# Moving the turned h and the list of further blocks in a mixture-of-experts loop

## The chip, the cores and the metric

The kernel runs on one core of a Trainium2 chip. The metric is the device time of one execution in microseconds (us). Before the change it is 3120.03 us, the median of three runs (3110.61, 3120.03 and 3121.97).

The engines have these names in the profile: PE is TensorE (matmuls; PEld its weight loads; PEq its sequencer, which takes instructions and branches), DVE is VectorE, ACT is ScalarE, POOL is GpSimd and SP is SyncE, which issues most DMAs here.

## The reference, cut to what matters

One block of a hybrid network over 2048 tokens of 1024 channels: a modulated norm, four token mixers side by side, their gated sum, and then a mixture of experts. Only the last part is touched by the change:

```
def hier_moe(h, rg_w, rg_b, re_w, re_b, w1, w3, w2):
    g_logits = hf @ rg_w + rg_b                     # 4 groups
    p_group = the softmax of the best group
    e_logits = (hf @ re_w + re_b) of that group     # 8 experts each
    top_v, top_i = lax.top_k(e_in, 2)
    w = p_group * softmax(top_v)
    return grouped_experts(h, expert ids, w, w1, w3, w2)

def expert_block(xb, e):                            # in blocks of rows of one expert
    return (silu(xb @ w1[e]) * (xb @ w3[e])) @ w2[e]   # 1024 -> 512 -> 1024

y[token] = the weighted sum over the token's two experts
out = rms_norm(x + gate * y)
```

There are 32 experts, and 2 x 2048 assignments of tokens to them, 128 for each on average. How many rows an expert gets is known only when the kernel runs.

## The kernel before, in words

The function `ffn` routes the tokens, makes for each expert the list of its rows (`idx`, `sct`) and their count (`cnt`), and then runs over the experts. The loop (L1053) is written out: 32 experts and one more pass that ends the last one. Matmuls that must be exact to fp32 are done in three passes: each operand is split into a high and a low part (`mhi` by ScalarE at L1294, `mlo` by VectorE at L1295), and `mm3` (L1434) issues low x high, high x low and high x high (L1438 to L1440).

The rows of an expert are worked in three sizes:

- The first 128 rows, always: gathered from `FR` (L869), turned by transposes (`parts`, L883), then `up` (48 matmuls into `ps_mm`), `silu`, `gate` (L928), turned again, and `down` (24 matmuls into `ps_sc`), whose result is multiplied at L949 and added to the output by an indirect DMA (L931).
- The next 64 rows, the *small block*, in two halves of 32, each behind a guard (`tc.If(count > 128 + 32 j)`): `up_rest` is its first product and `down_rest` its second (both `quarters`, matmuls at L958 into `ps_hf`, guard at L956); `placed_rest` multiplies (L987) and scatters behind the guard at L991. The guards are taken by TensorE and GpSimd (`ENGINES`). The count comes into their registers by `values_load` (L1038), two experts ahead.
- Rows beyond 192 of an expert go to a loop behind all experts (L1114), one block of 128 rows each. `beyond` (L1004 to L1032) makes the list of these blocks with VectorE alone.

The order in which the work of one pass of the loop is written, for expert e: [turned h of expert e-1: four transposes (L880), the copy of the high part by ScalarE (L891), the low part by VectorE (L892); split of w2 of expert e-1]; the load of the count of e+2; `up_rest`(e); `up`(e); silu; gate of the small block (L978) and its turning; turned rows of e+1; gate; gathers for e+2; `down`(e-1); `down_rest`(e); `placed_rest`(e). The helper `in_order` (L821) chains all instructions of TensorE, ScalarE and VectorE within the loop in that written order; so a step that is written earlier stands earlier on each of the three engines. DMAs, GpSimd's and SyncE's instructions are placed by the compiler's scheduler, and so is what stands ahead of the loop.

Weights stream in as panels of 128x1024 (`mraw`, 16 buffers; `mhi` and `mlo`, 12 each).

Of the kernel before, what the change touches and what calls it, by code (L numbers as in the profile page):

```python
# [4 lines left out]
F32 = mybir.dt.float32  # L5
F32R = mybir.dt.float32r
BF = mybir.dt.bfloat16
I32 = mybir.dt.int32
AF = mybir.ActivationFunctionType
OP = mybir.AluOpType  # L10
AX = mybir.AxisListType
# [550 lines left out]
NE, FF = 32, 512  # L562
CAP = 2048
NSLOT = 2
FIT = 192
# [5 lines left out]
def ffn(tc, G, A, out, bcast, rsqrt, split, mm3, MT, MR, X1, FR, mid):  # L571
    nc = tc.nc
# [4 lines left out]
    i32_ = rp.tile([128, 32], F32, name="i32_")  # L577
# [5 lines left out]
    cnt = rp.tile([128, 32], F32, name="cnt")  # L583
# [21 lines left out]
    with tc.tile_pool(reuse_waits="tile", name="wo", bufs=1, side="right") as wop, \  # L605
# [59 lines left out]
        def turned(i, x1, f, ss_, lg):  # L665
            fT = fTs[order.index(i) % 3].rearrange("p (k t) -> p k t", t=128)
            for c, o in enumerate(H):
                nc.vector.scalar_tensor_tensor(f[:, o], x1[:, o], ss_[:, 3:4], a4[:, o], op0=OP.mult, op1=OP.mult)
                nc.vector.tensor_add(f[:, o], f[:, o], m3[:, o])
                pt = psum("tr")  # L670
                for k in range(4):
                    nc.tensor.transpose(pt[:, k * 128:(k + 1) * 128], f[:, (4 * c + k) * 128:(4 * c + k + 1) * 128], G.ident)
                nc.scalar.copy(fT[:, 4 * c:4 * c + 4].rearrange("p k t -> p (k t)"), pt)
            for k in range(2):
                nc.sync.dma_start(FR[k * T + i * 128:k * T + (i + 1) * 128, 0:D], f)
            return fT, lg
# [119 lines left out]
        listed = assign(idx, sct, tab.rearrange("p s e -> p (s e)"), at, own)  # L796
# [16 lines left out]
    def parted(raw, eng=nc.vector):  # L813

        hi, lo = (wr.tile([128, 1024], F32R, name=n, bufs=PARTS) for n in ("mhi", "mlo"))
        split(raw, hi, lo, eng)
        return hi, lo, raw
# [3 lines left out]
    def in_order():  # L821

        traced = nc.cur_bb.bb.instructions
        if queues.get("block") is not traced:
            queues.clear()
            queues.update(block=traced, at=len(traced))
        for i in traced[queues["at"]:]:
            if i.engine in (mybir.EngineType.PE, mybir.EngineType.Activation, mybir.EngineType.DVE):
                if i.engine in queues:
                    tc.add_manual_dep(i, queues[i.engine].name, mybir.DependencyInfo(  # L830
                        mybir.DependencyClass.NoSync, mybir.DependencyReason.DATA), reason="in order")
                queues[i.engine] = i
        queues["at"] = len(traced)
# [13 lines left out]

    G.banks(mm=2, tr=2, sc=2, hf0=1, hf1=1)
    hu, hd = (psum(f"hf{i}") for i in range(2))
    for p in (hu, hd):  # L850
        nc.vector.memset(p, 0.0)

    xgs = [wr.tile([128, D + 1], F32, name=f"xg{r}") for r in (128, 64)]
    for i, x in enumerate(xgs):
# [28 lines left out]
    def parts(src, n, name):  # L883

        hi, lo = (wp.tile([128, n, 128], F32R, name=name + c) for c in "hl")
        out = []
        turned_into(lambda *a: out.append(a), src, 128, n)

        def taken():
            for c, v in out:  # L890
                nc.scalar.copy(hi[:, c], v)  # L891
                nc.vector.tensor_sub(lo[:, c], v, hi[:, c].bitcast(F32))  # L892
        return taken, (hi, lo)
# [8 lines left out]
    def weights(xg):  # L902
        w = wp.tile([128, 1], F32, name="w0", bufs=2)
        nc.scalar.copy(w, xg[:, D:D + 1])  # L904
        return w

    def weights_rest(xg):

        w = wp.tile([64, 2], F32, name="w1", bufs=2)
        for j, h in product(range(2), range(2)):  # L910
            nc.scalar.copy(w[h * 32:h * 32 + 32, j:j + 1], xg[j * 32:j * 32 + 32, D:D + 1])
        return w
# [67 lines left out]
    def down_rest(h, w2, guard):  # L980
        quarters(hd, 4, guard, lambda k, j: h[:, j * 2 + k % 2, (k // 2) * 32:(k // 2) * 32 + 32],
                 lambda k, g: w2[k][:, g * 256:g * 256 + 256])
# [19 lines left out]
    ovp = mo.enter_context(tc.tile_pool(reuse_waits="tile", name="ov", bufs=1))  # L1002

    def beyond():  # L1004

        J = -(-(CAP - FIT) // 128)
        ov = ovp.tile([128, 32], F32, name="ov")
        thr = ovp.tile([128, J], F32, name="thr")
        nc.vector.tensor_scalar(thr, i32_[:, :J], 128.0, float(FIT), op0=OP.mult, op1=OP.add)
        le = wp.tile([128, OVB, 32], BF, name="le", tag="mh1")  # L1010
        gt = le[:, :, :J]
        nc.vector.tensor_tensor(gt, cnt.unsqueeze(2).to_broadcast([128, 32, J]), thr.unsqueeze(1).to_broadcast([128, 32, J]),
                                op=OP.is_gt)
        nc.vector.tensor_reduce(ov, gt, axis=AX.X, op=OP.add)
        inc = ov
        for k in range(5):
            nxt = ovp.tile([128, 32], F32, name=f"inc{k}")
            nc.vector.tensor_copy(nxt[:, :1 << k], inc[:, :1 << k])
            nc.vector.tensor_add(nxt[:, 1 << k:], inc[:, 1 << k:], inc[:, :32 - (1 << k)])
            inc = nxt  # L1020
        nc.vector.tensor_tensor(le, inc.unsqueeze(1).to_broadcast([128, OVB, 32]),
                                i32_.unsqueeze(2).to_broadcast([128, OVB, 32]), op=OP.is_le)
        ej = ovp.tile([128, OVB], F32, name="ej")
        nc.vector.tensor_reduce(ej, le, axis=AX.X, op=OP.add)
        nc.vector.tensor_tensor(le, le, ov.unsqueeze(1).to_broadcast([128, OVB, 32]), op=OP.mult)
        bj = ovp.tile([128, OVB], F32, name="bj")
        nc.vector.tensor_reduce(bj, le, axis=AX.X, op=OP.add)
        nc.vector.tensor_sub(bj, i32_, bj)
        nc.vector.tensor_copy(ovt[:, 0:OVB], ej)
        nc.vector.tensor_copy(ovt[:, 2 * OVB:], inc[:, 31:32])  # L1030
        nc.vector.tensor_scalar(ej, ej, float(CAP), float(FIT), op0=OP.mult, op1=OP.add)
        nc.vector.scalar_tensor_tensor(ovf, bj, 128.0, ej, op0=OP.mult, op1=OP.add)  # L1032

    def fetch(e_, guard):
        return gather(idx[:, e_:e_ + 1], 0, nullcontext), gather(idx[0:64, NE + e_:NE + e_ + 1], 1, guard)
# [7 lines left out]
    out1, x1 = plain(rows_[1], 8, "xq", hd)  # L1043
    out0(), out1()
    w, w1 = weights(rows_[0]), weights_rest(rows_[1])
    rows_ = fetch(1, lambda: guards[1](0))
    sct4 = wr.tile([128, NE, 2], I32, name="sct4")
    for g, j in product(range(4), range(2)):
        nc.gpsimd.tensor_scalar(sct4[g * 32:g * 32 + 32, :, j], sct[j * 32:j * 32 + 32, NE:], 4.0, float(g), op0=OP.mult, op1=OP.add)
    with tc.issue_after(listed.ins):  # L1050
        w13 = [parted(t, nc.gpsimd if u < 2 else nc.vector) for u, t in enumerate(in_panels(0))]
    w2n = w2 = None
    for e_ in range(NE + 1):  # L1053
        in_order()
        more = e_ + 1 < NE
        q = nc.sync if e_ else nc.gpsimd
        if e_:

            turned, h = parts(h, 4, "h")
            turned()  # L1060
            in_order()
            w2, w2n = [parted(t) for t in w2n], None
            in_order()
        if e_ < NE:
            guard = guards[e_]
            if e_ + 2 < NE:
                guards.append(over(load(e_ + 2)))

            up_rest(x1, w13[:4], w13[4:], guard)
            pa = up(x, w13[:4], w13[4:])  # L1070
            in_order()
            raw = in_panels(e_ + 1, q) if more else []
            w2n = [loaded(A["e2"][e_][:, u], q) for u in range(4)]
            n13 = [parted(t) for t in raw[:4]]
            hn, h1 = silu(pa), silu_rest()
            in_order()
            gate_rest(h1, w1)
            out1, t1 = plain(h1, 4, "hq", hu)
            n13 += [parted(t) for t in raw[4:7]]
            out1()  # L1080
            if more:
                out0, x = parts(rows_[0], 8, "x")
                out1, x1 = plain(rows_[1], 8, "xq", hd)
                out0()
            in_order()
            gate(pa, hn, w)
            n13 += [parted(t) for t in raw[7:]]
            if more:
                out1()
                w, w1 = weights(rows_[0]), weights_rest(rows_[1])  # L1090
                if e_ + 2 < NE:
                    rows_ = fetch(e_ + 2, lambda: guards[e_ + 2](0))
            in_order()
        if e_:
            placed(down(h, [w2] * 2), sct[:, e_ - 1:e_], rest)
            in_order()
        if e_ < NE:
            down_rest(t1, w2n, guard)
            rest = placed_rest(guard, e_)
            in_order()  # L1100
            h, w13 = hn, n13
            if not more:
                beyond()


    fn, *e = [rp.tile([128, D], F32, name="mraw") for _ in range(RAW)]
# [7 lines left out]
    with tc.For_i(0, nov, 1) as it:  # L1114
# [4 lines left out]
        for k in range(2):  # L1119
            dlt = wp.tile([128, N], F32, name="ovd")  # L1120
            nc.vector.tensor_scalar(dlt, slot[k], sb, None, op0=OP.subtract)
            for i in range(N):
                P = wp.tile([128, 128], BF, name="ovP")
                for c in range(4):
                    nc.vector.tensor_scalar(P[:, c * 32:(c + 1) * 32], i32_, dlt[:, i:i + 1], float(-c * 32),
                                            op0=OP.subtract, op1=OP.is_equal)
# [10 lines left out]
        w2 = [InTurn(lambda u: dy("e2")[:, u], otiles) for _ in range(2)]  # L1137
# [5 lines left out]
        h = silu(pa)  # L1143
# [518 lines left out]
```

## Time and profile before

| | |
|---|---|
| median of three runs | 3120.03 us |
| profiled execution | 3115.34 us |
| its span (first to last instruction) | 3113.5 us |
| mean granted clock of TensorE | 0.958 |
| TensorE busy | 2822.9 us (91%) |
| VectorE busy | 1839.2 us (59%) |
| ScalarE busy | 1154.0 us (37%) |

The shares are means over stages with different limits. The stages from 0 to about 2223 us are the mixers and the router, which the change leaves as they are; from about 2223 to 3062 us run the loop's start, the 32 experts (some 25 us each) and the last `down`; after that the output is read again, normed and written. In a row of the order of time the first number is the start from the span's start, the second the duration, and the bracket at its end tells how long the engine stood before it and what it was waiting for.

### The profile page before, as it was taken

What the parts mean: (1) busy time and instruction counts of PE and PEld (TensorE: products, weight loads), DVE (VectorE), ACT (ScalarE), POOL (GpSimd) and SP (SyncE); (2) the same over time, 40 slices, a digit from 0 to 9 for tenths busy, and PEclk for the clock granted to TensorE, in tenths of its full rate; (3) what the DMA queues carried; (4) which work ended last, traced back from release to release, by engine and by line L of the source; (5) the groups of instructions that cost most, each with busy time, mean ns of one, the idle gap of its engine ahead of it and who ended that gap; (6) DMA issues with size and microseconds to landing.
All of it is one profiled execution on the core that took longest, in us unless ns stands there. A gap on an engine that the chain in (4) does not pass through costs nothing. (4 is left out here: it accounts for less than half of the span.)

```text
span 3113.5 us, 43212 instructions
## 1 busy us (share of the span) xinstructions
PE 2822.9 (91%) x15893; PEld 2229.4 (72%) x15893; DVE 1839.2 (59%) x2870; ACT 1154.0 (37%) x1722; POOL 574.3 (18%) x522
## 2 busy tenths in 40 slices
PE   7999999999967999899999999999688999999992
PEld 3887887787755677777777777887466767776671
DVE  4625125978776478523335333566588777787674
ACT  5411122322336133132222222322366566666552
POOL 3300010000004121013334333100211222111211
PEclk8999999999978899999999999999799999999996
DMA  7736254423118476866335433655698889998786
GB/s 288 252 111 214 80 166 146 155 86 95 68 43 267 130 213 195 268 230 236 122 125 181 160 115 133 195 177 162 198 331 296 287 291 299 307 319 289 251 270 232
DMA packets 245981, 621.46 MB, mean 200 GB/s; under 512 B 31128, under 2 KB 81464, under 8 KB 242008
## 3 DMA queue, kind: packets, MB, share of 16 engines
q1 hardware_dynamic: 211312, 506.17, 46.9%
q0 software_dynamic: 34416, 111.88, 12.8%
q8 instruction: 163, 2.67, 0.3%
q14 instruction: 90, 0.74, 0.1%
HBM read 484.86 MB, written 137.28 MB: 200 GB/s over the span
## 5 line engine op out<-in xcount | busy, mean ns | idle before, releaser
L1295 DVE TENSOR_TENSOR mlo<-mraw,mhi 128x1024 fp32r<-128x1024 f32 x382 | 450.2, 1225 | 58.5 <-ACT mhi L1294 53.0
L1294 ACT CAST mhi<-mraw 128x1024 fp32r<-128x1024 f32 x384 | 383.6, 1047 | 84.3 <-issue 44.7
L1438 PE MATMUL ps_mm<-hb1h,wlo 128*128 128x512 f32 x800 | 320.0, 400 | 3.7 <-DVE wlo L1295 3.7
L1440 PE MATMUL ps_mm<-hb1h,whi 128*128 128x512 f32 x800 | 318.3, 398 | 0.0
L1439 PE MATMUL ps_mm<-hb1l,whi 128*128 128x512 f32 x800 | 318.3, 398 | 0.0
L1589 ACT ACTIVATE ev<-ps_mm 128x512 f32<-128x512 f32 x128 | 76.2, 597 | 618.5 <-PE ps_mm L1440 515.6
L1295 DVE TENSOR_TENSOR wlo<-wraw,whi 128x1024 fp32r<-128x1024 f32 x164 | 217.2, 1333 | 142.6 <-ACT whi L1294 142.4
L1438 PE MATMUL ps_mm<-hb0h,wlo 128*128 128x512 f32 x672 | 269.5, 401 | 16.0 <-DVE wlo L1295 12.5
L1439 PE MATMUL ps_mm<-hb0l,whi 128*128 128x512 f32 x672 | 269.7, 401 | 0.0
L1440 PE MATMUL ps_mm<-hb0h,whi 128*128 128x512 f32 x672 | 267.8, 398 | 0.0
L1294 ACT CAST whi<-wraw 128x1024 fp32r<-128x1024 f32 x176 | 182.2, 1045 | 163.8 <-PE ps_mm L1440 70.0
L1438 PE MATMUL ps_mm<-mhi,xl 128*128 128x512 f32 x512 | 205.7, 402 | 24.5 <-PEq L956 24.2
L1639 POOL TENSOR_TENSOR macc<-macc,ev 128x512 f32<-128x512 f32 x96 | 167.1, 1740 | 307.0 <-DVE ev L1638 304.0
L1638 DVE TENSOR_TENSOR ev<-ev,ps_tr 128x512 f32<-128x512 f32 x96 | 65.8, 687 | 248.7 <-PE ps_tr L1440 243.8
L1439 PE MATMUL ps_mm<-mlo,xh 128*128 128x512 f32 x512 | 202.4, 395 | 3.2 <-ACT mhi L1294 2.4
L1440 PE MATMUL ps_mm<-mhi,xh 128*128 128x512 f32 x512 | 201.8, 394 | 1.4 <-issue 1.4
L1438 PEld LDWEIGHTS ps_mm<-hb1h,wlo 128*128 128x128 f32 x800 | 151.5, 189 | 38.2 <-DVE wlo L1295 4.1
L1440 PEld LDWEIGHTS ps_mm<-hb1h,whi 128*128 128x128 f32 x800 | 151.3, 189 | 33.1 <-issue 2.4
L1439 PEld LDWEIGHTS ps_mm<-hb1l,whi 128*128 128x128 f32 x800 | 151.4, 189 | 32.4 <-issue 1.9
L1438 PEld LDWEIGHTS ps_mm<-hb0h,wlo 128*128 128x128 f32 x672 | 127.7, 190 | 45.7 <-DVE wlo L1295 14.1
L869 POOL DMA_INDIRECT xg<-d_FR,idx x48 | 67.5, 1406 | 459.4 <-ACT w L904 444.1
L1439 PEld LDWEIGHTS ps_mm<-hb0l,whi 128*128 128x128 f32 x672 | 127.9, 190 | 29.5 <-issue 3.4
(592 smaller groups left out, 5861.0 us busy)
## 6 DMA issues: line engine op xcount, KB each, us to landing
mraw<-e SPq DMA_DIRECT2D x372, 512.0 KB
wraw<-wg SPq DMA_DIRECT2D x80, 512.0 KB
wraw<-wt SPq DMA_DIRECT2D x40, 512.0 KB
aw<-adaw SPq DMA_DIRECT2D x64, 256.0 KB
d_GS<-ev SPq DMA_DIRECT2D x64, 256.0 KB
ev<-d_GS POOLq DMA_DIRECT2D x64, 256.0 KB, 4.3
wraw<-wg POOLq DMA_DIRECT2D x24, 512.0 KB, 3.9
d_FR<-hb0h SPq DMA_DIRECT2D x22, 512.0 KB
```

Source lines behind the costliest of these rows:

```text
L869: nc.gpsimd.indirect_dma_start(out=xg, out_offset=None, in_=FR, in_offset=bass.IndirectOffsetOnAxis(ap=idx_ap, axis=0), bounds_check=2 * T ...
L1294: nc.scalar.copy(hi, raw)
L1295: eng.tensor_sub(lo, raw, hi.bitcast(F32))
L1438: nc.tensor.matmul(ps, wl, xh, start=start and n == 0, stop=False)
L1439: nc.tensor.matmul(ps, wh, xl, start=False, stop=False)
L1440: nc.tensor.matmul(ps, wh, xh, start=False, stop=stop and n == len(ks) - 1)
L1589: nc.scalar.activation(g, ps, AF.Sigmoid)
L1638: nc.vector.tensor_mul(g, g, ps)
L1639: nc.gpsimd.tensor_add(acc, acc, g)
```

## The change

Three things are moved, and one is written in another way:

- The clearing of the two `ps_hf` banks by VectorE is put behind the list of rows for the gather (`listed`).
- `beyond` is called beside the first gather, ahead of the loop, instead of behind the last expert. It counts an expert's further blocks by an addition, a maximum and a shift of integers, where it compared the count with 15 thresholds and summed.
- The turned h of expert e is made ahead of `down_rest`(e), in the same pass, where it was made at the start of the next one. The split of w2 stays at the start of the next pass; for the last expert it is made right behind its gate.

Lines of the changed kernel are one further than before in most of this function.

```diff
--- before.py
+++ after.py
@@ -847,8 +847,9 @@
 
     G.banks(mm=2, tr=2, sc=2, hf0=1, hf1=1)
     hu, hd = (psum(f"hf{i}") for i in range(2))
-    for p in (hu, hd):
-        nc.vector.memset(p, 0.0)
+    with tc.issue_after(listed.ins):
+        for p in (hu, hd):
+            nc.vector.memset(p, 0.0)
 
     xgs = [wr.tile([128, D + 1], F32, name=f"xg{r}") for r in (128, 64)]
     for i, x in enumerate(xgs):
@@ -1003,15 +1004,12 @@
 
     def beyond():
 
-        J = -(-(CAP - FIT) // 128)
+        ovi = ovp.tile([128, 32], I32, name="ovi")
+        nc.vector.tensor_scalar(ovi, cnt, float(127 - FIT), 0.0, op0=OP.add, op1=OP.max)
+        nc.vector.tensor_single_scalar(ovi, ovi, 7, op=OP.arith_shift_right)
         ov = ovp.tile([128, 32], F32, name="ov")
-        thr = ovp.tile([128, J], F32, name="thr")
-        nc.vector.tensor_scalar(thr, i32_[:, :J], 128.0, float(FIT), op0=OP.mult, op1=OP.add)
+        nc.vector.tensor_copy(ov, ovi)
         le = wp.tile([128, OVB, 32], BF, name="le", tag="mh1")
-        gt = le[:, :, :J]
-        nc.vector.tensor_tensor(gt, cnt.unsqueeze(2).to_broadcast([128, 32, J]), thr.unsqueeze(1).to_broadcast([128, 32, J]),
-                                op=OP.is_gt)
-        nc.vector.tensor_reduce(ov, gt, axis=AX.X, op=OP.add)
         inc = ov
         for k in range(5):
             nxt = ovp.tile([128, 32], F32, name=f"inc{k}")
@@ -1043,6 +1041,7 @@
     out1, x1 = plain(rows_[1], 8, "xq", hd)
     out0(), out1()
     w, w1 = weights(rows_[0]), weights_rest(rows_[1])
+    beyond()
     rows_ = fetch(1, lambda: guards[1](0))
     sct4 = wr.tile([128, NE, 2], I32, name="sct4")
     for g, j in product(range(4), range(2)):
@@ -1056,10 +1055,9 @@
         q = nc.sync if e_ else nc.gpsimd
         if e_:
 
-            turned, h = parts(h, 4, "h")
-            turned()
-            in_order()
-            w2, w2n = [parted(t) for t in w2n], None
+            if e_ < NE:
+                w2p = [parted(t) for t in w2n]
+            w2 = w2p
             in_order()
         if e_ < NE:
             guard = guards[e_]
@@ -1085,6 +1083,8 @@
             in_order()
             gate(pa, hn, w)
             n13 += [parted(t) for t in raw[7:]]
+            if not more:
+                w2p = [parted(t) for t in w2n]
             if more:
                 out1()
                 w, w1 = weights(rows_[0]), weights_rest(rows_[1])
@@ -1095,12 +1095,13 @@
             placed(down(h, [w2] * 2), sct[:, e_ - 1:e_], rest)
             in_order()
         if e_ < NE:
+            turned, h = parts(hn, 4, "h")
+            turned()
+            in_order()
             down_rest(t1, w2n, guard)
             rest = placed_rest(guard, e_)
             in_order()
-            h, w13 = hn, n13
-            if not more:
-                beyond()
+            w13 = n13
 
 
     fn, *e = [rp.tile([128, D], F32, name="mraw") for _ in range(RAW)]
```

On TensorE this is the boundary between two experts (about 30 such pieces are alike). First before: `ps_sc` is the `down` of the expert before, `ps_hf<-mraw,hq` the second product of the small block, `ps_tr<-c_kid,mh` the turning of h, `cnti` the load of the count, `ps_hf<-mraw,xq` the first product of the next small block.

```order
L1440 MATMUL ps_sc<-mhi,hh 128x512
L956 COMPARE_AND_BRANCH
L958 MATMUL ps_hf_16947<-mraw,hq 32x256 x16
L956 COMPARE_AND_BRANCH
L958 MATMUL ps_hf_16947<-mraw,hq 32x256 x16
L956 UNCONDITIONAL_BRANCH x3
L991 COMPARE_AND_BRANCH x2
L991 UNCONDITIONAL_BRANCH x4
L880 MATMUL ps_tr<-c_kid,mh_17559 128x128 x4
L1038 TENSOR_LOAD cnti
L1038 ISA x2
L956 COMPARE_AND_BRANCH
```

And the same piece after:

```order
L1441 MATMUL ps_sc<-mhi,hh 128x512
L881 MATMUL ps_tr<-c_kid,mh_17591 128x128 x4
L957 COMPARE_AND_BRANCH
L959 MATMUL ps_hf_16947<-mraw,hq 32x256 x16
L957 COMPARE_AND_BRANCH
L959 MATMUL ps_hf_16947<-mraw,hq 32x256 x16
L957 UNCONDITIONAL_BRANCH x3
L992 COMPARE_AND_BRANCH x2
L992 UNCONDITIONAL_BRANCH x4
L1036 TENSOR_LOAD cnti
L1036 ISA x2
L957 COMPARE_AND_BRANCH
```

The four transposes have moved from between the guards to right behind `down`; the guards of the second product (L957), of the scatter (L992) and of the next first product (L957) now stand with only the load of the count between them. Nothing else has moved on this engine.

On VectorE this is the end of the last expert. Before, the list of further blocks (`le`, `ej`, `bj`, `ovt`, `ovf`) stands between the small block's multiply and the low part of h (`hl`), with the split of the last weights (`mlo`) behind:

```order
L1025 TENSOR_TENSOR le<-le,ov 128x1024
L1027 TENSOR_REDUCE bj<-le 128x32
L1028 TENSOR_TENSOR bj<-i__14714,bj 128x32
L1029 CAST ovt<-ej 128x32
L1030 CAST ovt<-inc_27529 128x1
L1031 TENSOR_SCALAR ej<-ej 128x32
L1032 SCALAR_TENSOR_TENSOR ovf<-bj,ej 128x32
L892 TENSOR_TENSOR hl<-ps_tr,hh 128x512
L1295 TENSOR_TENSOR mlo<-mraw,mhi 128x1024 x4
L949 TENSOR_TENSOR my_27594<-ps_sc,m_16956 128x512 x2
```

After, with the gate of the last expert (L929) at the start:

```order
L929 SCALAR_TENSOR_TENSOR mh_27460<-ps_mm,w_27234,mh_27460 128x512
L1296 TENSOR_TENSOR mlo<-mraw,mhi 128x1024 x4
L957 UNCONDITIONAL_BRANCH
L950 TENSOR_TENSOR my_27515<-ps_sc,m_16956 128x512 x2
L893 TENSOR_TENSOR hl<-ps_tr,hh 128x512
L988 TENSOR_TENSOR my_27562<-ps_hf_16947,m5x 128x512
L992 UNCONDITIONAL_BRANCH
L950 TENSOR_TENSOR my_27594<-ps_sc,m_16956 128x512 x2
```

The list is gone from here, the split of the last weights stands right behind the gate, and `hl` ahead of the small block's multiply (L988).

On VectorE at the start of the loop, before: the clearing of two banks (L851) stands ahead of the cast to `idx`, the list that the first gather reads.

```order
L800 CAST cnti<-cnt 128x32
L851 MEMSET ps_hf_16946 128x512
L594 TENSOR_SCALAR at<-tab 128x64
L851 MEMSET ps_hf_16947 128x512
L595 TENSOR_TENSOR tab<-tab,at 128x64
L596 CAST idx<-tab 128x64
L597 TENSOR_SCALAR at<-tab 128x64
L598 TENSOR_TENSOR tab<-tab,at 128x64
L599 TENSOR_TENSOR sct<-tab,own 128x64
L892 TENSOR_TENSOR xl<-ps_tr,xh 128x512 x2
```

After:

```order
L800 CAST cnti<-cnt 128x32
L594 TENSOR_SCALAR at<-tab 128x64
L595 TENSOR_TENSOR tab<-tab,at 128x64
L596 CAST idx<-tab 128x64
L597 TENSOR_SCALAR at<-tab 128x64
L852 MEMSET ps_hf_16946 128x512
L598 TENSOR_TENSOR tab<-tab,at 128x64
L852 MEMSET ps_hf_16947 128x512
L599 TENSOR_TENSOR sct<-tab,own 128x64
L1008 TENSOR_SCALAR ovi<-cnt 128x32
L1009 TENSOR_SCALAR ovi<-ovi 128x32
L1011 CAST ov<-ovi 128x32
```

The cast to `idx` (L596) has moved up by both clearings, and the first steps of the list of further blocks follow behind `sct`; its last steps stand behind `xl`, among the first splits of weights.

## Rows read from the trace of the kernel before

**Rows 1.** The head of the page: span and instructions.

```profile
span 3113.5 us, 43212 instructions
```

**Rows 2.** Stretch 2280:3040; busy us of PE, PEld, DVE, ACT, POOL, clock, DMA.

```profile
2280.00:3040.00 760.00, 704.43 (x4699) 537.82 (x4699) 578.75 (x628) 473.18 (x714) 148.20 (x92) 0.99 0.87 290
```

**Rows 3.** Waits of PE there: us in total, times, longest.

```profile
PE ps_mm L1438 <- PEq L956: 22.1, 26, 4.4
PE ps_tr L880 <- DVE my L987: 11.9, 10, 1.2
PE ps_tr L880 <- PEq L956: 9.2, 16, 0.6
```

**Rows 4.** Order of time, PE, a boundary with both small blocks skipped.

```profile
2359.61 0.63 PE L880 MATMUL ps_tr<-c_kid,mh 128*128 128x128 f32 x4 [0.56 <-PEq L956]
2360.92 0.47 PE L1438 MATMUL ps_mm<-mhi,xl 128*128 128x512 f32 x1 [0.68 <-PEq L956]
```

**Rows 5.** PE's sequencer there by line: ns min/median/max, first and last start.

```profile
L956 PEldq EVENT_SEMAPHORE  x2: 51/51/51, 2359.1 to 2360.8; - x2
L956 PEldq COMPARE_BRANCH  x1: 433/433/433, 2360.3 to 2360.3; - x1
...
L991 PEldq COMPARE_BRANCH  x1: 208/208/208, 2359.2 to 2359.2; - x1
...
L880 PEldq EVENT_SEMAPHORE  x1: 51/51/51, 2359.5 to 2359.5; - x1
...
L1038 PEldq TENSOR_LOAD <-cnti x1: 303/303/303, 2359.6 to 2359.6; - x1
```

**Rows 6.** Order of time, PE, a boundary with half of the second product.

```profile
2336.66 0.63 PE L880 MATMUL ps_tr<-c_kid,mh 128*128 128x128 f32 x4 [1.20 <-DVE my L987]
2338.53 0.77 PE L1438 MATMUL ps_mm<-mhi,xl 128*128 128x512 f32 x1 [1.24 <-PEq L956]
```

**Rows 7.** Order of time, PE, behind a second product run in full.

```profile
2597.10 0.47 PE L1438 MATMUL ps_mm<-mhi,xl 128*128 128x512 f32 x1 [0.98 <-PEq L956]
```

**Rows 8.** Stretches with and without the lower clock, columns as in rows 2.

```profile
2338.40:2341.70 3.30, 3.17 (x8) 2.52 (x9) 2.92 (x4) 3.30 (x4) 0.10 (x1) 0.50 1.02 241
...
2360.90:2372.00 11.10, 11.08 (x48) 8.92 (x48) 10.63 (x11) 10.65 (x13) 0.73 (x1) 1.00 0.89 258
```

**Rows 9.** The guards' branches at L956 on PE's sequencer, 2280:3040.

```profile
L956 PEldq COMPARE_BRANCH  x119: 65/179/4174, 2283.5 to 3036.4; - x119
```

**Rows 10.** Order of time, PE and DVE, the end of the last expert.

```profile
3040.64 1.93 PE L958 MATMUL ps_hf<-mraw,hq 128*32 128x256 f32 x32
...
3052.87 0.77 PE L1438 MATMUL ps_sc<-mhi,hl 128*128 128x512 f32 x1 [8.57 <-DVE hl L892]
...
3061.25 0.40 PE L1440 MATMUL ps_sc<-mhi,hh 128*128 128x512 f32 x1
...
3043.34 0.16 DVE L1009 TENSOR_SCALAR thr<-i__14714 128x15 f32<-128x15 f32 x1
...
3048.89 1.23 DVE L1025 TENSOR_TENSOR le<-le,ov 128x1024 bf16<-128x1024 bf16 x1
...
3052.04 0.68 DVE L892 TENSOR_TENSOR hl<-ps_tr,hh 128x512 fp32r<-128x512 f32 x1
```

**Rows 11.** Order of time, DVE, PE and POOL, the start of the loop.

```profile
2224.19 0.48 DVE L851 MEMSET ps_hf<- 128x512 f32 x1
...
2236.76 0.69 DVE L892 TENSOR_TENSOR xl<-ps_tr,xh 128x512 fp32r<-128x512 f32 x1 [10.43 <-ACT xh L891]
...
2234.99 1.97 PE L880 MATMUL ps_tr<-c_kid,xg 128*128 128x128 f32 x8 [11.34 <-DMA xg<-d_FR,idx]
...
2241.44 2.40 POOL L1295 TENSOR_TENSOR mlo<-mraw,mhi 128x1024 fp32r<-128x1024 f32 x1
```

**Rows 12.** Order of time, PE, transposes that wait for a gated h.

```profile
2266.51 1.09 PE L880 MATMUL ps_tr<-c_kid,mh 128*128 128x128 f32 x4 [4.67 <-DVE mh L928]
...
2301.09 0.43 PE L880 MATMUL ps_hf<-c_kid,mh 64*128 64x64 f32 x4 [0.21 <-DVE mh L978]
```

## The prediction, made before the changed kernel was run

> **What bounds the kernel now.** The change touches the loop over the 32 experts and what stands just ahead of it and behind it, some 840 us of a span of 3113.5 us [rows 1]. I first read the table by stretches for the loop [rows 2]: of 760 us TensorE's matmuls are busy 704.43, VectorE 578.75, ScalarE 473.18, and the granted clock is 0.99. So TensorE sets the pace there, and what matters is the 55 us in which it stands. The list of its waits [rows 3] says for whom: 22.1 us before the first matmul of an expert, 9.2 and 11.9 us before the four transposes of h; nearly all of it is put down to its own sequencer at the guard's branch (L956) or to the multiply at L987 behind that branch. No weight and no gather appears in those rows. What TensorE gets more to do, or waits longer, therefore adds straight to the time.
>
> The order of time shows what such a wait consists of, at a boundary where both small blocks are skipped [rows 4]. The last matmul of the old expert ends at 2359.05 (2359.61 less 0.56); the transposes follow 0.56 us later; the first matmul of the next expert starts at 2360.92, 0.68 us behind them. The sequencer's rows [rows 5] tell why. At a guard whose body is skipped it waits until the matmuls issued before have ended. From 2359.1 on it then works in series: the scatter's guard (L991, 0.208 us), a wait of 0.051 us for the transposes (L880), the load of the next count (L1038, 0.303), the next guard (L956, 0.433). The transposes run from 2359.61 to 2360.24 **beside** the load of the count and what follows it: they cost the boundary nearly nothing. From the last matmul to the first it is 1.87 us, all of it that chain of the sequencer.
>
> **The transposes, part by part.** The change puts them ahead of the guard of the small block's second product. Then the sequencer must wait at that guard until they have ended too, and the same chain starts afterwards, with nothing beside it. The pair of neighbouring guards does not save one of the waits: between them stand the guard of the scatter and the load of the count, and it is their series that fills the time.
> - Added: the four transposes take 0.63 us, and a matmul here starts some 0.17 before the one ahead of it ends (it lasts 0.40 us, as the one at 3061.25 in [rows 10], and one starts every 0.231, which is 11.08 us over 48 in the last row of [rows 8]). That is 0.46 us.
> - Taken off: the wait for them leaves the chain, 0.051 us and about as long for issuing it; I take 0.13.
> - Net 0.33 us a boundary. The bounds are 0 (if the load of the count turns out to run beside the transposes as now) and 0.63 (nothing overlaps).
>
> It goes for 30 boundaries. The 16 waits for L956 in [rows 3] are those where the second product was skipped, the 10 for L987 those where half of it ran, and the other four ran in full. Where half ran [rows 6], TensorE stands twice, 1.20 us before the transposes and 1.24 behind them; where all of it ran [rows 7] only behind them, 0.98. In the first of these the transposes again lie within the sequencer's chain, since the branch of the second half is skipped; in the second they are issued without a pause, but the load of the count runs beside them. So both lose the same cover. 30 x 0.33 = **+9.9 us**.
>
> At the first boundary (expert 0) the transposes wait for the gated h [rows 12] and start at 2266.51; the next matmul came 0.20 us behind them, as the guards had been passed meanwhile. Now the guards come after them: their 1.09 us, then the chain of 1.87 - 0.13 = 1.74, gives 2269.34 in place of 2267.80, **+1.5**. Against it, VectorE has the low part of h done earlier, ahead of L987, so the small block's gate may be ready when TensorE asks for it: five waits of 0.2 us (one in [rows 12]), **-1.0** at most; I take that.
>
> **The clock.** The granted clock is 1.00 (2.4 GHz) through most of the loop. Behind the half-run boundary of [rows 6], after 2.4 us of standing with only the transposes between, it is 0.50 (1.2 GHz) from 2338.4 to 2341.7 [rows 8]; so it is in two more places, at 2488.6 and 2918.7, both behind such a boundary. Eight matmuls took that 3.30 us, where the rate at full clock makes it 8 x 0.231 = 1.85: 1.45 us for each. Three of ten half-run boundaries had it. With the transposes gone from the middle, TensorE stands there in one piece of over 2 us, and I expect the fall at six or seven of the ten: 3.5 x 1.45 = **+5.1**. The bounds are 0 and 7 x 1.45 = 10.2.
>
> **The list of further blocks.** In the tail VectorE computes it from 3043.34 to 3052.04 [rows 10], and only then the low part of the last h, for which TensorE waits 8.57 us; the 24 matmuls behind it then start at half the clock and end at 3061.65. After the change h is turned ahead of the second product, and the list is long done. Transposes 0.46 ahead of the product: this ends at 3040.64 + 1.93 + 0.46 = 3043.03. Behind it about the gap that stands there now, 1.07, then 24 x 0.231 + 0.17 = 5.7 us at full clock: 3049.8. **-11.8 us**. The weights of that last product must be split earlier, right behind the gate; if they come late the gain is nearer to the 8.7 us of the list alone, which is its lower bound. The rows that follow (scatter, reload, norm) move with it.
>
> **The start.** VectorE clears two banks (0.48 us each in [rows 11], 0.40 from start to start) ahead of the list of rows that the first gather waits for, and TensorE waits 11.34 us for that gather. Both go behind it: **-0.8**. The new place of the list of further blocks is VectorE's idle 10.43 us before 2236.76, where the larger part of its 8.7 us fits. What stands behind that, a product over 32 x 32 (1.23 us in [rows 10]), a sum over it of about the same and a few small steps, is some 2.8 us, among the first splits of weights. The second split, on GpSimd, ends only at 2243.84 [rows 11], and I take it that TensorE waits for that one anyway: 0. Without that cover it costs up to 2.8, so this part lies between -0.8 and +2.0.
>
> **Sum.** -11.8 - 0.8 + 9.9 + 1.5 - 1.0 + 5.1 = +2.9 us on the profiled execution's 3115.34. That execution is 4.7 us faster than the median of the three runs, 3120.03; put on that, 3120.0 + 2.9 = 3122.9, say **3123 us**. All terms at their lower ends would give 3106.4, all at their upper ends 3144; they will hardly go there together, and I give this case 3109 to 3136.
>
> **Rivals.**
> - *The loop pays nothing.* The load of the count keeps running beside the transposes, or the sequencer is faster through two guards in a row; only tail and start are left: 3120.0 - 12.6 = 3107.4. For it: the chain in [rows 5] has gaps of 0.1 us between steps that no row explains. Against it: in [rows 4] the wait at the guard ends 0.04 us after the last matmul, so it does hold the sequencer.
> - *One of the two waits goes.* If neighbouring guards really leave one stand where there were two, the 0.56 us of [rows 4] goes at each of 30: 17 us less than the case above, 3090. Against it: the steps of [rows 5] are all still there.
> - *The clock falls at the skipped boundaries too* (slower). At the 15 boundaries where the second product is skipped and less than all of the next first product runs, TensorE now stands twice for about 0.6 us; afterwards once, for 1.74. That is nearer to the 2 us and more behind which the clock was seen to fall. If it falls at eight of these and at all ten half-run ones: 8 x 1.45 + 3.5 x 1.45 = 16.7 us more than my sum, 3140. It decides from about eight such places. For it: the fall in [rows 8] came after 2.44 us of standing in two pieces. Against it: the 1.87 us of [rows 4] with the transposes inside were followed by 1.00 (last row of [rows 8]).
> - *A jump waits for code.* One branch of 119 took 4.174 us where the median is 0.179 [rows 9], and it was followed by a stretch at half the clock. Two skipped bodies in a row are a longer jump; three more such branches would cost 3 x (4.17 - 0.43 + 1.45) = 15.6 us: 3138.5. Against it: the jumps keep their lengths, and only four instructions move.
>
> The Trainium skill ("Runtime: NRT & Kernel Launch", section on instruction fetch) says that a taken branch whose target is outside the two pages held makes the engine fetch the page before it goes on. The one branch of 4.174 us in [rows 9] agrees with it, the median of the 119 shows no such stall, and no run here shows where the pages lie. By that rule the last rival's price would be paid wherever the shift puts a jump across a page's edge, and by the row it has happened once in 119.
>
> **Chances.** My forecast 0.58; the loop pays nothing 0.18; one wait goes 0.07; the clock 0.12; code 0.05. A measurement of this kernel can tell about 0.5%, 15.6 us, from no change: under 3104.4 is faster, over 3135.6 slower. Faster: the case of one wait and a quarter of the case beside it, 0.12. Slower: clock and code but for a third of them, which fall short of the line, and a little of my own case: 0.16. The same: 0.72. The range takes in most of the clock's and code's cases above and the loop that pays nothing below: 3102 to 3141 (my own case 3109 to 3136).
>
> **What would show it.** In the profile after, at a skipped boundary: the transposes directly behind the old expert's last matmul, then one gap of 1.7 to 1.8 us put down to the guard, and 2.1 to 2.4 us from last matmul to first. At half-run boundaries one gap over 2 us, and more stretches at 0.50. TensorE's waits before L1438 then hold nearly all of the 43 us of [rows 3], and more. In the tail the 8.57 us are gone and the last 24 matmuls run at full clock. If the gap at a skipped boundary is 1.2 us or less, the sequencer does not pay for the order, and the time comes out near 3107 or below; if the tail still has a wait over 2 us, the list or the last weights came late.

## The result, and the profile after

The changed kernel took 3135.44 us (median of 20 runs, 3122.96 to 3144.57), the kernel before 3122.48 beside it (20 runs): ratio 1.0051, 95% interval [1.0038, 1.0064]. That is 13 us slower by the medians and some 16 by the ratio, which is estimated from all runs and is not the quotient of the two medians. The forecast was 3123, that is +2.9 us, in a range of 3102 to 3141. The profiled execution took 3136.72 us, 21.4 more than that of before; 3.3 us of this are there already at the router's last matmul, ahead of everything the change touches.

First the table by stretches of the loop, columns as in [rows 2]:

```profile
2280.00:3040.00 760.00, 686.26 (x4507) 530.65 (x4505) 569.30 (x616) 473.18 (x702) 136.57 (x90) 0.97 0.87 287
```

TensorE is busy 18 us less in the same 760 us, at a mean clock of 0.97 in place of 0.99. Its waits there (us in total, times, longest), to be read against [rows 3]:

```profile
PE ps_mm L1439 <- PEq L957: 43.9, 25, 6.0
PE ps_hf L959 <- ACT mhi L1295: 15.3, 6, 3.3
PE ps_hf L959 <- ACT hh L892: 10.8, 8, 1.5
```

The waits ahead of the transposes are gone, and those ahead of the next product have grown by more. The lines on L959 name ScalarE, but they are the same stand before the next expert's first matmul, where that is one of the small block's. A skipped boundary, in order of time (before: [rows 4]):

```profile
2366.52 0.60 PE L881 MATMUL ps_tr<-c_kid,mh 128*128 128x128 f32 x4
2368.88 0.47 PE L1439 MATMUL ps_mm<-mhi,xl 128*128 128x512 f32 x1 [1.76 <-PEq L957]
```

The transposes follow `down` without a pause, and then TensorE stands once, for 1.76 us. A half-run boundary, after (before: [rows 6]):

```profile
2339.70 1.93 PE L959 MATMUL ps_hf<-mraw,hq 128*32 128x256 f32 x32
2344.92 0.76 PE L1439 MATMUL ps_mm<-mhi,xl 128*128 128x512 f32 x1 [3.29 <-PEq L957]
```

That is 3.29 us in one piece, where it was 1.20 and 1.24 with the transposes between. The sequencer's load of the count at this boundary (ns), first before, then after:

```profile
L1038 PEldq TENSOR_LOAD <-cnti x1: 795/795/795, 2336.8 to 2336.8; - x1
```

```profile
L1036 PEldq TENSOR_LOAD <-cnti x1: 1195/1195/1195, 2342.7 to 2342.7; - x1
```

From the last matmul of `down` to the first of the next expert this boundary took 4.93 us before and takes 5.59 after; the longer load is 0.40 of these 0.66 us. Whether the order made it longer, these two traces can't tell. Where nothing is run it takes 0.30 us in both traces. Behind a half-run body it took 0.58 to 0.80 us in the trace before and 1.06 to 1.24 in the trace after (one 1.46), behind a body run in full 0.91 to 1.11 and 1.41 to 1.55.

The stretches at half the clock (PE busy us, granted clock, DMA share, GB/s; three of twelve in the loop, before there were five):

```profile
2344.00:2347.40 3.40, 2.48 (x6) 0.50 0.98 258
...
2634.10:2637.50 3.40, 2.95 (x7) 0.50 1.06 228
...
2736.50:2739.90 3.40, 3.27 (x8) 0.50 1.00 301
```

Eight of the twelve stand behind half-run boundaries (three before). At the first boundary, of expert 0, in order of time, then the guard's branch, then the DMA queues between 2268.9 and 2272.8 us (packets, MB, share):

```profile
2266.85 1.08 PE L881 MATMUL ps_tr<-c_kid,mh 128*128 128x128 f32 x4 [4.81 <-DVE mh L929]
2272.84 0.76 PE L1439 MATMUL ps_mm<-mhi,xl 128*128 128x512 f32 x1 [4.91 <-PEq L957]
```

```profile
L957 PEldq COMPARE_BRANCH  x1: 3581/3581/3581, 2269.1 to 2269.1; - x1
```

```profile
q8 instruction: 1, 0.02, 1.7%
```

The branch took 3.58 us, and one packet of instructions arrived while it stood. The tail (before: [rows 10]):

```profile
3073.19 1.93 PE L959 MATMUL ps_hf<-mraw,hq 128*32 128x256 f32 x32
3076.25 0.50 PE L1439 MATMUL ps_sc<-mhi,hl 128*128 128x512 f32 x1 [1.12 <-DVE my L988]
...
3081.70 0.40 PE L1441 MATMUL ps_sc<-mhi,hh 128*128 128x512 f32 x1
```

The wait of 8.57 us is gone and the last 24 matmuls run at full clock. From the end of expert 30's `down` to the end of expert 31's it was 20.94 us (3040.71 to 3061.65) and is 9.26 (3072.83 to 3082.09).

Added up between the two traces: from the second expert's first matmul to the last expert's, +27.1 us (16 skipped boundaries +6.7, of which 1.6 at one place by a branch of 1.82 us; ten half-run +8.5; four in full +2.4; the 48 matmuls of each first product +10.5 by the lower clock; the rest -1.1); the tail -11.7. With +3.3 ahead of all that, +0.2 at the start, +1.5 at expert 0 and +0.9 behind the last matmul this is the 21.3 us between the two spans.

### The profile page after: what moved, and what is told of

Its sections match the earlier page's. It is cut to its first block, busy times and chain, and to the rows that moved or that the text cites. A ratio compares the mean times of both kernels' runs of the same rounds, so it can differ in the third digit from the quotient of the medians.

```text
span 3134.8 us, 43302 instructions
## 1 busy us (share of the span) xinstructions
PE 2829.5 (90%) x15893; PEld 2243.3 (72%) x15893; DVE 1834.6 (59%) x2870; ACT 1158.5 (37%) x1722; POOL 569.7 (18%) x522
## 5 line engine op out<-in xcount | busy, mean ns | idle before, releaser
L1439 PEld LDWEIGHTS ps_mm<-mhi,xl 128*128 128x128 f32 x512 | 101.2, 198 | 86.5 <-issue 65.8
```

The source lines that it names most:

```text
L1439: nc.tensor.matmul(ps, wl, xh, start=start and n == 0, stop=False)
```

## The experiments

Each ratio is to the kernel before, run beside it. The experiments were run in three groups of four kernels (a "call" in the expectations), each group on one chip and the three on three chips; the kernel before took 3142.13, 3140.21 and 3137.85 us on them. For the first comparison and its two traces the chip is not on record, and three of its twenty runs of the kernel before are those of the opening. A ratio can differ from the quotient of the medians: for list_only that would be 0.9960. The two kernels that were run for a trace alone, before_again and before_third, took 3143.87 and 3135.47 us.

| kernel | median us | ratio | 95% interval |
|---|---|---|---|
| changed, first comparison | 3135.44 | 1.0051 | 1.0038 to 1.0064 |
| list_only | 3129.68 | 0.9976 | 0.9959 to 0.9993 |
| turn_only | 3143.16 | 1.0003 | 0.9986 to 1.0021 |
| load_early | 3099.41 | 0.9867 | 0.9842 to 0.9892 |
| list_load | 3100.27 | 0.9873 | 0.9846 to 0.9900 |
| after_again | 3138.86 | 0.9981 | 0.9962 to 1.0000 |
| turn_twice | 3132.76 | 0.9969 | 0.9954 to 0.9984 |
| load_twice | 3182.14 | 1.0132 | 1.0110 to 1.0154 |
| after_third | 3140.13 | 1.0008 | 0.9989 to 1.0026 |
| split_load | 3092.10 | 0.9861 | 0.9836 to 0.9887 |
| split_turn | 3094.88 | 0.9865 | 0.9838 to 0.9892 |

**list_only and turn_only: the change in two halves.** In the first, the pass starts again as before:

```
+            turned, h = parts(h, 4, "h")
+            turned()
+            in_order()
+            w2, w2n = [parted(t) for t in w2n], None
...
-            turned, h = parts(hn, 4, "h")
-            turned()
```

In the second the clearing of the banks and `beyond` are as before, and only the turned h is moved.

> The changed kernel with the turned h back at its old place; the list of further blocks and the clearings stay moved. Theory A (the new place of the turned h makes the loop longer, list and start only gain): the tail's 8.57 us wait is gone, the loop is as before, ratio to the kernel before about 0.996 (-12 us). Rival B (the list beside the first gather, or something else at the start, is what costs): at or over 1.004.

> The kernel before with the turned h alone moved (and the last w2 split behind the gate); the list stays behind the last expert. Theory A: the loop is about 30 us longer as in the profile after, the tail some 9 us shorter since only the last multiplies wait for the list: ratio 1.006 to 1.008. Rival B: 0.998 or less, the tail's gain without the start's cost.

The list alone gains 0.24% by the ratio, some 7 us, and 12 us by the medians; the expected 0.996 lies at the edge of the interval. Its tail, in order of time:

```profile
3053.32 0.66 PE L881 MATMUL ps_tr<-c_kid,mh 128*128 128x128 f32 x4 [1.46 <-DVE my L988]
3055.65 0.80 PE L1435 MATMUL ps_sc<-mhi,hl 128*128 128x512 f32 x1 [1.67 <-ACT mhi L1291]
3056.91 0.79 PE L1436 MATMUL ps_sc<-mlo,hh 128*128 128x512 f32 x1 [0.46 <-DVE mlo L1292]
```

The 8.57 us are now 1.67, but the late weights keep some of it, and the first eleven of the 24 matmuls still run at half the clock (most of them 0.63 us each instead of 0.40). turn_only shows the other side, with the list (`thr`) still behind the last expert and a wait as short as the changed kernel's 1.12:

```profile
3056.35 0.50 PE L1442 MATMUL ps_sc<-mhi,hl 128*128 128x512 f32 x1 [1.07 <-DVE thr L1009]
```

From the last expert's first matmul to its last it takes 26.6 us, as the changed kernel does; list_only takes 31.9 and the kernel before 38.3. So most of the tail's gain comes from turning h, and splitting the last weights, earlier. The list's own move is worth about 2.7 us more behind the last matmul (55.4 us to the end in turn_only, 52.8 in the changed kernel). Rival B is out. The turned h alone was to be 0.6 to 0.8% slower and is not distinguishable from the kernel before; so theory A, as it stood, was wrong on this chip. The trace of either kernel is from the fastest of its 12 runs. In both traces the loads behind a body take 1.14 to 1.58 us, with either place of the turned h. That led to theory E.

**before_again, after_again, before_third, after_third: the two kernels themselves, on two more chips.**

> The kernel before itself, for its trace on the chip of these runs. Theory E (the load of the count behind a run body depends on the chip or its state, not on the order): if the loads behind a body take over 1.1 us in the other kernels of this call, they do so here too, the half-run gaps sum to over 3 us and most are followed by a granted clock of 0.50. Theory F (they are longer because the turned h does not stand ahead of the load): here 0.6 to 1.1 us, as in the first trace.

> The changed kernel itself beside the kernel before on one chip. Theory E: where the loads behind a body are long in both, the change costs only the 0.33 us a boundary and gains the tail, ratio 0.999 to 1.003; where they are short in the kernel before, 1.004 or more. Theory F: 1.004 to 1.006 on any chip.

> The kernel before once more, for its trace on the chip of these runs. Theory E: the loads of the count behind a run body are as long as in the changed kernel's trace of this call, whichever length that is. Theory F: 0.4 us shorter than there.

> The changed kernel beside the kernel before once more. Ratio by what the trace of the kernel before shows behind a half-run body: 1.003 or more where its loads take 0.6 to 0.8 us and few falls of the clock follow; 0.997 to 1.001 where they take 1.4 us or more and most of these boundaries are followed by 0.50 in both kernels.

The same half-run boundary on the third of those chips, kernel before, in order of time, and its load:

```profile
2729.55 0.63 PE L880 MATMUL ps_tr<-c_kid,mh 128*128 128x128 f32 x4 [1.73 <-DVE my L987]
2731.90 0.47 PE L1438 MATMUL ps_mm<-mhi,xl 128*128 128x512 f32 x1 [1.73 <-PEq L956]
```

```profile
L1038 PEldq TENSOR_LOAD <-cnti x1: 1446/1446/1446, 2729.6 to 2729.6; - x1
```

And the changed kernel there:

```profile
2737.11 0.77 PE L1439 MATMUL ps_mm<-mhi,xl 128*128 128x512 f32 x1 [3.53 <-PEq L957]
```

```profile
L1036 PEldq TENSOR_LOAD <-cnti x1: 1484/1484/1484, 2734.7 to 2734.7; - x1
```

Here the load is as long in the kernel before, and moving the turned h costs this boundary nothing: over ten half-run boundaries -2.3 and -0.7 us on these two chips, against +8.5 in the first two traces. The skipped boundaries cost the same more everywhere: a median of 0.31, 0.30 and 0.32 us. The whole change is 0.9981 and 1.0008 there. Behind half-run bodies theory E holds in these traces and F does not: the loads take 1.29 to 1.56 us with the old place of the turned h and 1.29 to 1.54 with the new one. Behind a body run in full they stay somewhat shorter with the old place (medians of 1.17 and 1.35 us against 1.48 and 1.47). One sign that was given with theory E did not come: in before_third only four of the ten half-run boundaries lose the clock (eight in before_again, eight and seven in the changed kernel).

From the second expert's first matmul to the last expert's the kernel before took 755.6, 779.7 and 772.6 us in its three traces, the changed kernel 782.6, 786.8 and 783.0; the tail is 11.7, 12.0 and 11.6 us shorter. So it is the kernel before that was short in the first pair. Its medians say the same: 3122 us in the first comparison and 3138 to 3142 on the other chips, against 3135 to 3140 for the changed kernel. That agrees with short loads in the former alone, but rests on one trace of it. Theory E by itself does not explain the first comparison: if both kernels stood on one chip there, something made the loads of one longer than those of the other (0.58 to 0.80 against 1.06 to 1.46 us), and whether that was the order is not shown.

**load_early and list_load: the load of the count elsewhere.** Both have

```
-            if e_ + 2 < NE:
-                guards.append(over(load(e_ + 2)))
...
                 if e_ + 2 < NE:
+                    guards.append(over(load(e_ + 2)))
                     rows_ = fetch(e_ + 2, lambda: guards[e_ + 2](0))
```

the first on the changed kernel, the second on list_only.

> The changed kernel with the load of the count (two experts ahead) moved from between the guards to just ahead of the gathers. Theory A (a boundary is the series of steps of TensorE's sequencer behind the drained guard): the load's 0.3 us and its 0.2 us of register work go at 16 skipped boundaries and 1.1 to 1.5 us more at the 14 with a body run, about -25 us, and fewer falls of the clock, -5 to -10: ratio to the kernel before about 0.994. Rival D (the time behind a run body is not the load's own but a wait for something else that has to end): the branch behind takes the load's place, ratio stays near 1.002 to 1.005.

> The turned h at its old place, list and clearings moved, load of the count ahead of the gathers. Theory A: -12 us of the list, 0.5 us less at skipped boundaries and 0.6 to 1 us less at the others, about -20, and fewer falls of the clock, -5: ratio about 0.988. Rival D: 0.996, as with the list alone.

All loads of load_early in the loop (ns, minimum, median, maximum):

```profile
L1036 PEldq TENSOR_LOAD <-cnti x29: 297/304/316, 2285.0 to 2979.9; - x29
```

None is long any more, and the two kernels are 1.3% faster than the kernel before, with either place of the turned h; rival D is out. Part of this is the list and the tail. The load's own price is read from list_load against list_only, on one chip: 29 us by the medians, 0.9%, the largest single price found at the boundaries. load_early was expected at 0.994 and gained twice as much; 0.994 is the 1.0051 of the first comparison less the expected 30 to 35 us, and the changed kernel is nearer to 1.000 on the other chips. With the load away, the old place is the better one at a skipped boundary. list_load, in order of time:

```profile
2355.42 0.63 PE L881 MATMUL ps_tr<-c_kid,mh 128*128 128x128 f32 x4 [0.56 <-PEq L957]
2356.20 0.47 PE L1433 MATMUL ps_mm<-mhi,xl 128*128 128x512 f32 x1
...
2368.07 0.43 PE L881 MATMUL ps_hf<-c_kid,mh 64*128 64x64 f32 x4 [0.74 <-DVE mh L979]
```

What is left of the chain ends with the transposes. But the small block's gate is then late, 0.74 us here and 6.9 us over eleven places, since the low part of h stands ahead of it on VectorE: the time comes back there, and the two kernels end level.

**load_twice: the suspected cost doubled.**

```
             if e_ + 2 < NE:
+                load(e_ + 2)
                 guards.append(over(load(e_ + 2)))
```

> The changed kernel with the count loaded twice in a row at the same place (the first value is not used). Theory A: 0.30 + 0.15 us and two small gaps more at each skipped boundary, 0.55 us, 30 x 0.55 = +17 us and some more falls of the clock: +20 to 30 on the changed kernel. If the long load behind a body waits for something that ends, the second load takes 0.30 there; if the load itself is slow at that time, both take over 1 us and the cost is +30 to 40.

It cost 43 us on the changed kernel of the same group (3182.14 against 3138.86), above the upper end of what was expected. At a half-run boundary the two loads (ns) took

```profile
L1036 PEldq TENSOR_LOAD <-cnti x2: 438/869/1300, 2350.0 to 2351.7; - x2
```

1.30 and then 0.44 us: the first waits for something that ends, and the second hardly does. Skipped boundaries now stand 2.4 us, and seven of eight with no small block on either side were followed by a first product of 12.6 to 12.8 us in place of 11.15, that is, by half the clock; the loop has 23 such stretches.

**turn_twice: the stand cut in two.**

```
+                pd = psum("tr")
+                for k in range(4):
+                    nc.tensor.transpose(pd[:, k * 128:(k + 1) * 128], hprev[:, k * 128:(k + 1) * 128], G.ident)
```

> The changed kernel with four more transposes of the same h at the old place, ahead of the load of the count (their result is not read). Theory A: they lie in the shadow of the sequencer's chain, which grows only by their wait, +0.1 to 0.15 us a boundary, +4 us; the stand behind a half-run body is in two pieces again. If the fall of the clock hangs on one piece, it comes after fewer of them and the time is 3 to 8 us below the changed kernel's; if on the sum, as many and +4 us. Theory F: the loads behind a body are 0.4 us shorter than in the changed kernel's trace of this call.

```profile
2372.64 0.66 PE L1061 MATMUL ps_tr<-c_kid,mh 128*128 128x128 f32 x4 [0.46 <-PEq L957]
2373.96 0.47 PE L1444 MATMUL ps_mm<-mhi,xl 128*128 128x512 f32 x1 [0.66 <-PE ps_tr L1061]
```

With four transposes more at each boundary the kernel was 6 us faster than after_again in the medians, but the intervals of the two ratios overlap, so a gain is not shown. By the two traces the boundaries cost 2.3 us more and the first products 12.3 less; the loop has eight stretches at 0.50 in place of thirteen. The trace of after_again is from the slowest of its 12 runs. The loads behind a body stay at 1.30 to 1.58 us, which is against F once more.

**split_load and split_turn: the guards of gather and scatter on GpSimd alone,** with the early load.

```
-    load = lambda e_: nc.values_load(cnti[0:1, e_:e_ + 1], engines=ENGINES, min_val=0, max_val=CAP)
+    load = lambda e_, g: nc.values_load(cnti[0:1, e_:e_ + 1], engines=[g], min_val=0, max_val=CAP)
...
-            rest = placed_rest(guard, e_)
+            rest = placed_rest(there[e_], e_)
```

> As the kernel with the old place of the turned h and the early load, and the counts are loaded for TensorE and GpSimd apart, so that the guards of the gather and the scatter stand on GpSimd alone. Theory A (every step of the sequencer behind the drained guard is paid): 0.21 us and a gap go at skipped boundaries, about 0.5 us where a half runs, some -10 us more: ratio about 0.984. Rival: TensorE waits for the drain and the transposes anyway, 0.987.

> The same on the kernel with the new place of the turned h and the early load: now the two guards stand next to each other with nothing between. Theory A: 0.25 us less at skipped boundaries and 0.5 us at half-run ones, ratio about 0.983, within 0.2% of the kernel with the old place, since the transposes lie in a stand at the old place and the stand is shorter at the new one. Rival (the new place pays once the guards are true neighbours): 0.4% or more below the kernel with the old place.

Both ratios are about that of the early load alone; some 10 us more were expected, and the interval of split_load would still allow it. In the traces the loop did become shorter, 728.3 us against list_load's 749.8 and 735.8 against load_early's 747.6. But the stretch from the first expert's first matmul to the second's became longer (31.3 us against 25.4, and 34.1 against 29.5), and the trace of split_load is from the fastest of its six runs. The branches left had become slower at many places. At one skipped boundary of split_load:

```profile
L957 PEldq COMPARE_BRANCH  x1: 1532/1532/1532, 2354.9 to 2354.9; - x1
```

Twelve branches of over 0.8 us sum to 22.9 us there, against seven and 17.4 in list_load and four and 11.2 in the kernel before, and each of the twelve has a packet of 16384 bytes on the instruction queue while it stands or just ahead. True neighbours gain nothing over the old place (0.9865 against 0.9861).

## Why the prediction was right, and where it was not

The time came out within the range and 12 us above the value, and still under the 3136 of the forecast's own case by 0.6 us, which is luck: the change was put at +2.9 us and came out at +13. In the first pair of traces every term but the start's had the sign that was forecast, and the mechanism was right at a skipped boundary and in the tail. Step by step:

- *Skipped boundaries*: +0.33 us forecast, a median of 0.32, 0.31 and 0.30 in three pairs of traces; one stand of 1.76 us as described. Right: the turned h lost its cover, and neighbouring guards save no stand.
- *Half-run and full boundaries*: the same 0.33 was taken, since "both lose the same cover". This is the step that was mis-sized. The first pair has +0.85 and +0.60 on average, the other two about -0.1 to -0.2 and +0.2 to +0.3. Some 1.7 us of the first pair's +8.5 at half-run boundaries are the lower clock in first products of the small block (an estimate, from three such stretches after and two before). The load of the count was given its 0.3 us everywhere; behind a run body it takes 0.6 to 1.6, and the 0.795 us that it took at the boundary of [rows 6] did not enter the sum. The trace of [rows 6] has it shorter than any other trace of a load at that place.
- *The clock*: six or seven of ten half-run boundaries were forecast, eight fell, and four more places with them (before: two). The first products took 10.5 us more, where 5.1 was forecast; in the other two pairs it was 4.8 and 7.3. The cost of one (1.45) held: the first products spent 23.8 us more at 0.50, that is seven stretches of 3.4 us, for 10.5 us. The reason that was given, the stand in one piece, is not shown: in before_again eight fell too, where TensorE stood 3.2 us with the transposes between. load_twice shows the rival's mechanism: skipped boundaries do lose the clock, at 2.4 us of standing, and mostly not at the 1.76 of the change.
- *Expert 0*: +1.5 was forecast and +1.5 came, by other terms. The branch of 3.58 us costs 3.2 more; it is in all three traces of the changed kernel (3.58, 2.98 and 3.50) and at that place in none of before. The wait for the small block's gate ahead of it fell by 3.7. So the rival of code happened in part: once at this place, and a branch of 1.82 us at a skipped boundary came in this trace alone. The packet at expert 0 agrees with the Trainium skill ("Runtime: NRT & Kernel Launch", section on instruction fetch), by which a taken branch out of the pages held waits for the page.
- *Small block's gates*: -1.0 forecast, the five waits went, and the rest of the loop is -1.1.
- *Tail*: -11.8 forecast, -11.7 measured, by the path described.
- *Start*: the first gather's wait went from 11.34 to 10.69 us, -0.65 for -0.8; a slower branch at the first product took that back.

The likeliest case, no change that can be told, is what two of three comparisons show (0.9981 and 1.0008); in the first, the one that was forecast, the kernel was 0.5% slower, clear of the noise, and by its two traces the term of the run bodies and the clock that follows them made the difference.

What stays open: what the load waits for behind a run body, and why it was short in the one trace of the kernel before. The packets of instructions don't explain it: about two thirds of the long loads in the six traces of the two kernels have none within 1.5 us.

## What to carry to other kernels

Where an engine's sequencer waits for its engine to drain, as TensorE's does here at a skipped guard, the steps behind that wait are paid in series; put register loads where the engine still has work queued (0.9% here). Small matmuls cost little inside such a stand and their own time ahead of it (0.3 us a skipped boundary here), but look at what else then becomes late. Take the price of a step from each kind of place where it occurs, not from the cheapest. A difference of half a per cent measured once need not hold on another chip: repeat it, with a trace of both kernels, before building on its sign.

## What the runs showed of the hardware

- A register load on TensorE's sequencer took 0.30 us with no guarded body ahead, and 0.58 to 1.58 behind one, by run; a second load right behind took 0.30 to 0.44.
- With four idle transposes more in each stand the loop had eight stretches at 1.2 GHz where thirteen were, by one trace each; that this pays in time is not shown.
- With two guards less on TensorE others were slower: nine branches of 1.1 to 1.5 us in split_load, each with a packet of 16384 bytes of instructions during it or just ahead. That the shorter run of code is the cause is not shown.
- The same kernel took 3122 us in one comparison and 3138 to 3142 on three chips, and a change's ratio was 1.0051, 0.9981 and 1.0008.
